# Pooling sums and most of the branch gating of a gated mixer on POOL instead of DVE

## The chip, the cores and the metric

One core of one Trainium2 chip (trn2) runs the whole program in a single launch. The metric is the time of an execution in device microseconds; of several runs the median is taken. The engines are named as in the profile: PE does the matrix products (its weight loads, PEld, run beside them), DVE and ACT are the two elementwise engines that can read PE's accumulators, POOL is the third elementwise engine, and SP issues most of the DMAs. Each engine takes its own instructions strictly in the order in which they stand in its queue, and waits for other engines by semaphores.

## The reference, cut to what matters

The model is two blocks on a sequence of 512 rows of 1024 numbers in fp32. The first (two layers of mixers, cross attention and a feed-forward net) isn't touched. The second has two layers; each is a mixer of three branches and a feed-forward net:

```
proj = h @ w_in[l]
q, k, v, f_logit, cx, cb, cc, px, gate_logit = split(proj)
y_attn = forgetting_attention(q, k, v, f_logit) @ w_attn_out[l]
y_conv = short_conv_mixer(cx, cb, cc, conv_w[l]) @ w_conv_out[l]
# pooling, for each of four groups of 64 features, window w = 2, 4, 8, 16:
#   d = (sum of the last w rows of px) / min(t + 1, w) - px
#   y_pool[group] = (d @ w_grp) * pool_scale
g = sigmoid(gate_logit)            # three gates of 1024 features
merged = g[0] * y_attn + g[1] * y_conv + g[2] * y_pool
x = x + merged @ w_o[l]
```

## The kernel before

Features lie on the 128 partitions and the 512 rows of the sequence along them, so a tile of 128 x 512 is 128 features of the whole sequence. Every product is done in three passes: both factors are split into a high part (rounded, by ACT, line 160) and a low part (the rest, by DVE, line 161), and PE adds high x high, high x low and low x high. So every block of weights that comes from memory costs ACT a cast and DVE a subtraction before PE can use it. The products with the large gate weights go by Strassen's scheme with seven products instead of eight (`seven`, `plan_seven`); that costs DVE four more additions of 128 x 1024 for each pair of blocks (line 469). A `Feed` keeps the splits of some four units of weights ahead of PE.

A layer's mixer (`mixer2`) runs attention heads first, with the short convolution's products between them, then:

- `pooling` (lines 1525 to 1559): the product for 256 features in two halves (`ft`). ACT copies a half out of the accumulator (`pu`, L1534). The window sums are built by doubling: `step` copies the first k columns and adds the tile to itself shifted by k (L1539, L1540). The first half (windows 2 and 4) needs two such steps, the second (8 and 16) four. Then follow a copy of 64 partitions (L1545, L1551), the division by the count (L1552 for the first 16 columns, L1553 for the rest) and the subtraction of the input (L1554). The result is split for the next product: the high part by ACT (L1558, two instructions of 64 partitions), the low part by DVE (L1559, two).
- `gates` (from line 1389): eight products of six matmuls each for the convolution's branch, whose accumulators ACT copies into `m` (L1440). Accumulators of this kind (tag `at`) have four buffers. Then `pool_conv` for each of four pairs of feature tiles: seven products for two gates, the sigmoids on ACT (L1456, L1444, L1445), the product of `m` with its gate (L1457), the pooled branch (two matmuls, L1454 and L1455, read by L1459) and its addition to `m` (L1461), the three of them on DVE. After the second and the fourth pair comes the attention branch (`attn`).

A scheduler orders the instructions of each engine by data dependences and by its own estimate of how long each takes; the program text alone does not set the order on ACT and DVE.

Of the kernel before, what the change touches and what calls it, by code (L numbers as in the profile page):

```python
# [15 lines left out]
ALU = mybir.AluOpType  # L16
# [5 lines left out]
S = 512  # L22
# [74 lines left out]
class Core:  # L97
# [1291 lines left out]
    def gates(self, mp, bt, l, w, aT, ds, ch, cl):  # L1389

        nc, a = self.nc, self.a
        v = nc.vector
        self.extra, self.turn = mp, 0

        self.T.append(mp.tile([P, 8, 256], F32R, name=self.nm("t4"), bufs=1))
        for i, (hi, lo) in enumerate(((self.Hh[:, 0:4, 256:], self.Hl[:, 0:4, 256:]),
                                      (self.T[2][:, 0:4, :], self.T[2][:, 4:8, :]))):
            b = self.block(mp, None, "rb").rearrange("p (k c) -> p k c", k=4)
            nc.sync.dma_start(out=b, in_=self.td[:, i])
            self.split(hi, lo, b)  # L1400

        ah = mp.tile([P, 4, S], F32R, name=self.nm("ah"), bufs=1)
        al = mp.tile([P, 4, S], F32R, name=self.nm("al"), bufs=1)
        mp.tile([P, 16], F32, name=self.nm("gap"), bufs=1)
        self.split(ah, al, aT)
        ms = [self.big(3), self.big(0)]
        m = [ms[f // 4][:, f % 4, :] for f in range(8)]
        feed = Feed()

        def src(g, fb, r):  # L1410
            c0 = 2568 + g * D + fb * 256
            return w[r * 512:r * 512 + 512, c0:c0 + 256]

        def pool_unit(fb):
            raw, hi, lo = [self.wp.tile([P, 1024], d, tag=t, name=self.nm("w"), bufs=n) for d, t, n in
                           ((F32, "raw", 3), (F32R, "whi", 5), (F32R, "wlo", 5))]
            for r in range(0, P, 64):
                nc.sync.dma_start(out=raw[r:r + 64, :256], in_=a["pool_w_2"][l, fb])
            self.split(hi[:, :256], lo[:, :256], raw[:, :256])
            return hi, lo  # L1420

        for fb in range(4):
            feed.put(lambda fb=fb: self.unit(a["w_conv_out_2"][l][:, fb * 256:fb * 256 + 256], 2, 256))
        for fb in range(4):
            feed.put(lambda fb=fb: pool_unit(fb))
            self.plan_seven(feed, mp, lambda i, r, fb=fb: src(1 + i, fb, r))
            if fb % 2:
                self.plan_seven(feed, mp, lambda i, r, fb=fb: src(0, fb - 1 + i, r))
                for i in range(2):
                    feed.put(lambda f=fb - 1 + i: self.unit(  # L1430
                        a["w_attn_out_2"][l][:, f * 256:f * 256 + 256], 4, 256))
        for i in range(4):
            feed.put(lambda i=i: self.unit(a["w_o_2"][l][i * 256:i * 256 + 256, 0:S], 2, S))

        for fb in range(4):
            u = feed.get()
            for c in range(2):
                p = self.at_tile()
                self.gemm_a(p, [u], c * P, ch, cl)
                nc.scalar.copy(out=m[fb * 2 + c], in_=p)  # L1440

        def second(a_, u):
            sg = bt.tile([P, S], F32, tag="sg", name=self.nm("sg"))
            nc.scalar.activation(out=sg[:, :256], in_=a_, func=AF.Sigmoid)  # L1444
            nc.scalar.activation(out=sg[:, 256:], in_=u, func=AF.Sigmoid)  # L1445
            return sg

        def pool_conv(fb):
            hi, lo = feed.get()

            def end(c, g, a_, u):
                f = fb * 2 + c
                p = self.at_tile()
                nc.tensor.matmul(p, lhsT=hi[:, c * P:(c + 1) * P], rhs=ds[:, fb, :], start=True, stop=False)  # L1454
                nc.tensor.matmul(p, lhsT=lo[:, c * P:(c + 1) * P], rhs=ds[:, fb, :], start=False, stop=True)  # L1455
                nc.scalar.activation(out=g, in_=g, func=AF.Sigmoid)  # L1456
                v.tensor_tensor(out=m[f], in0=m[f], in1=g, op=ALU.mult)  # L1457
                sg = second(a_, u)
                v.scalar_tensor_tensor(out=sg, in0=p, scalar=self.vec("psc", l * 8 + f), in1=sg,  # L1459
                                       op0=ALU.mult, op1=ALU.mult)  # L1460
                v.tensor_tensor(out=m[f], in0=m[f], in1=sg, op=ALU.add)  # L1461

            self.seven(feed, mp, end)

        def attn(fb, last):
            sgs = []

            def end(c, g, a_, u):
                nc.scalar.activation(out=g, in_=g, func=AF.Sigmoid)
                sgs.append((g, second(a_, u)))  # L1470

            self.seven(feed, mp, end)
            for i in range(2):
                un = feed.get()
                for c in range(2):
                    f = (fb + i) * 2 + c
                    p = self.at_tile()
                    self.gemm_a(p, [un], c * P, ah, al)
                    sg = sgs[c][i]
                    v.tensor_tensor(out=sg, in0=p, in1=sg, op=ALU.mult)  # L1480
                    v.tensor_tensor(out=m[f], in0=m[f], in1=sg, op=ALU.add)
                    if last:
                        self.split(self.Hh[:, f, :], self.Hl[:, f, :], m[f])

        for fb in range(4):
            pool_conv(fb)
            if fb % 2:
                attn(fb - 1, fb == 3)
        for f in range(4):
            self.split(self.Hh[:, f, :], self.Hl[:, f, :], m[f])  # L1490
        self.extra = None
        return [feed.get(5) for _ in range(4)]
# [32 lines left out]
    def pooling(self, bt, w, pool, ds):  # L1525

        nc = self.nc
        v = nc.vector
        us = self.units_a(w, 2312)
        for ft in range(2):  # L1530
            p = self.mm_tile()
            self.gemm_a(p, us, ft * P, self.Hh, self.Hl)
            u = bt.tile([P, S], F32, tag="cx", name=self.nm("pu"))
            nc.scalar.copy(out=u, in_=p)  # L1534
            s = bt.tile([P, S], F32, tag="sg", name=self.nm("psum"))
            s2 = bt.tile([P, S], F32, tag="sg", name=self.nm("cy"))

            def step(dst, src, k, lo):
                v.tensor_copy(out=dst[lo:, 0:k], in_=src[lo:, 0:k])  # L1539
                v.tensor_tensor(out=dst[lo:, k:], in0=src[lo:, k:], in1=src[lo:, :S - k], op=ALU.add)  # L1540

            if ft == 0:
                step(s, u, 1, 0)
                step(s2, s, 2, 64)
                v.tensor_copy(out=s[64:, :], in_=s2[64:, :])  # L1545
            else:
                step(s, u, 1, 0)
                step(s2, s, 2, 0)
                step(s, s2, 4, 0)
                step(s2, s, 8, 64)  # L1550
                v.tensor_copy(out=s[64:, :], in_=s2[64:, :])  # L1551
            v.tensor_tensor(out=s[:, :16], in0=s[:, :16], in1=pool[:, ft, :16], op=ALU.mult)  # L1552
            v.tensor_scalar(out=s[:, 16:], in0=s[:, 16:], scalar1=pool[:, ft, 16:17], scalar2=None, op0=ALU.mult)  # L1553
            v.tensor_tensor(out=s, in0=s, in1=u, op=ALU.subtract)  # L1554
            for e in range(2):
                r, o = slice(e * 64, e * 64 + 64), slice(64 - e * 64, 128 - e * 64)
                hi = ds[r, ft * 2 + e, :]
                nc.scalar.copy(out=hi, in_=s[r])  # L1558
                v.tensor_tensor(out=ds[o, ft * 2 + e, :], in0=s[r], in1=hi.bitcast(F32), op=ALU.subtract)  # L1559
# [162 lines left out]
```

## Time and profile before

| | us |
|---|---|
| median of three runs | 2978.25 (2976.13 to 2985.57) |
| the profiled execution's own time | 2976.68 |
| its span, first to last instruction | 2974.8 |
| PE busy | 2942.1 (99%) |
| DVE busy | 2259.5 (76%) |
| ACT busy | 1505.3 (51%) |
| POOL busy | 74.8 (3%) |

Times within the profile are counted from the first instruction. An engine's busy time is the time in which it had an instruction in work. Where a row ends in square brackets, these hold the idle time before it and what ended that. The second block's two mixers are alike: what stands at 1721 us in the first layer stands at 2425 us in the second.

### The profile page before, as it was taken

The page shows a single profiled execution, that of the slowest core. Times are in us where ns is not written, and L with a number is a line of the kernel's source. Part 1 is how long each engine was busy: PE and PEld are TensorE (multiplying, and loading weights), DVE is VectorE, ACT ScalarE, POOL GpSimd, SP SyncE. Part 2 cuts the span into 40 slices and gives each one's busy share as a digit, 9 for nine tenths or more (in the row PEclk, how much of TensorE's full clock was granted, in tenths as well). Part 3 has the DMA queues.
Part 4 walks back from the last instruction along what each step waited for, and adds up shares of the span by engine and source line. Part 5 has one row for each costly group of instructions (what it writes and reads, how often), then busy time and mean ns, then how long its engine had stood idle before and what let it go on. Part 6 is the DMA issues. An engine that isn't in the chain of part 4 may idle for free.

```text
span 2974.8 us, 46959 instructions
## 1 busy us (share of the span) xinstructions
PE 2942.1 (99%) x18312; PEld 2594.8 (87%) x18312; DVE 2259.5 (76%) x4266; ACT 1505.3 (51%) x2469; POOL 74.8 (3%) x113
## 2 busy tenths in 40 slices
PE   8999999999999999999999999999999999999999
PEld 6878889999988788999988789899998779999998
DVE  6855767988777576798879688697777778787775
ACT  6634545555444454555545465454444555454442
POOL 1300000000000000000001000000000000000000
PEclk9999999999999999999999999999999999999999
DMA  5122522343332353233335233423334324423332
GB/s 178 43 86 94 176 85 79 114 121 92 105 109 79 127 170 98 71 109 121 97 102 142 75 116 97 159 83 121 93 102 134 110 79 124 135 93 107 100 108 78
DMA packets 233955, 320.65 MB, mean 108 GB/s; under 512 B 11077, under 2 KB 166199, under 8 KB 232837
## 3 DMA queue, kind: packets, MB, share of 16 engines
q1 hardware_dynamic: 224933, 292.20, 31.5%
q0 software_dynamic: 8800, 25.45, 2.8%
q8 instruction: 144, 2.36, 0.3%
q14 instruction: 78, 0.64, 0.1%
HBM read 297.63 MB, written 15.78 MB: 105 GB/s over the span
## 4 chain that ended last, share of the span: by engine, by line
PE 88%; DVE 7%; ACT 2%; DMA 2%; issue 1%; SPq 0%; POOL 0%; DVEq 0%; ACTq 0%
PE mm L245 61%; PE at L245 19%; PE at L196 3%; DVE wl L161 2%; DVE wr L469 1%; PE at L1340 1%; DMA wr<-in_ffn_w_in 1%; DMA wr<-in_w_in 1%; PE at L1202 1%; ACT wh L160 1%; PE at L700 0%; PE at L857 0%; PE at L1624 0%; PE at L1626 0%; DVE x L548 0%
## 5 line engine op out<-in xcount | busy, mean ns | idle before, releaser
L161 DVE TENSOR_TENSOR wl<-wr,wh 128x1024 fp32r<-128x1024 f32 (+1 forms) x678 | 817.9, 1213 | 297.0 <-ACT wh L160 284.5
L160 ACT CAST wh<-wr 128x1024 fp32r<-128x1024 f32 (+1 forms) x678 | 702.4, 1044 | 581.5 <-PE mm L245 238.8
L245 PE MATMUL mm<-Hh,wh 128*128 128x256 f32 (+1 forms) x2256 | 678.1, 301 | 4.0 <-DVE g L518 3.7
L245 PE MATMUL mm<-Hh,wl 128*128 128x256 f32 (+1 forms) x2256 | 674.5, 299 | 0.0
L245 PE MATMUL mm<-Hl,wh 128*128 128x256 f32 (+1 forms) x2256 | 673.7, 299 | 0.0
L245 PEld LDWEIGHTS mm<-Hh,wh 128*128 128x128 f32 x2256 | 424.5, 188 | 24.1 <-DVE g L518 4.8
L245 PEld LDWEIGHTS mm<-Hl,wh 128*128 128x128 f32 x2256 | 425.4, 189 | 18.5
L245 PEld LDWEIGHTS mm<-Hh,wl 128*128 128x128 f32 x2256 | 424.9, 188 | 17.5 <-issue 0.3
L245 PE MATMUL mm<-wh,Hh 128*128 128x512 f32 x896 | 359.4, 401 | 0.8 <-ACT Hh L160 0.6
L245 PE MATMUL mm<-wl,Hh 128*128 128x512 f32 x896 | 354.1, 395 | 2.1 <-DVE ss L321 2.0
L245 PE MATMUL mm<-wh,Hl 128*128 128x512 f32 x896 | 353.8, 396 | 0.0
L245 PE MATMUL mm<-big,wh 128*128 128x256 f32 x1920 | 334.1, 277 | 1.7 <-DVE u L530 1.7
L245 PEld LDWEIGHTS mm<-big,wh 128*128 128x128 f32 x1920 | 289.6, 188 | 2.4 <-DVE u L530 2.3
L469 DVE TENSOR_TENSOR wr<-wr,wr 128x1024 f32<-128x1024 f32 x208 | 253.7, 1220 | 49.8 <-DMA wr<-in_w_ffn_in 25.2
L245 PE MATMUL at<-wh,al 128*128 128x512 f32 x704 | 277.4, 394 | 0.0
L245 PE MATMUL at<-wl,ah 128*128 128x512 f32 x704 | 276.1, 392 | 0.0
L245 PE MATMUL at<-wh,ah 128*128 128x512 f32 x704 | 273.8, 389 | 0.0
L245 PE MATMUL mm<-big,wl 128*128 128x256 f32 x960 | 265.6, 277 | 0.0
L245 PEld LDWEIGHTS mm<-wl,Hh 128*128 128x128 f32 x896 | 169.6, 189 | 38.0 <-DVE wl L161 3.3
L245 PEld LDWEIGHTS mm<-wh,Hl 128*128 128x128 f32 x896 | 169.3, 189 | 38.1 <-DVE Hl L161 1.3
L245 PEld LDWEIGHTS mm<-wh,Hh 128*128 128x128 f32 x896 | 169.4, 189 | 36.2 <-ACT Hh L160 1.2
L245 PEld LDWEIGHTS mm<-big,wl 128*128 128x128 f32 x960 | 180.2, 188 | 0.3 <-DVE wl L161 0.2
(403 smaller groups left out, 4268.2 us busy)
## 6 DMA issues: line engine op xcount, KB each, us to landing
wr<-in_ffn_w_in SPq DMA_DIRECT2D x88, 512.0 KB
wr<-in_w_ffn_in SPq DMA_DIRECT2D x88, 512.0 KB
wr<-in_w_in SPq DMA_DIRECT2D x84, 512.0 KB
wr<-in_ffn_w_out SPq DMA_DIRECT2D x44, 512.0 KB
wr<-in_w_ffn_out SPq DMA_DIRECT2D x44, 512.0 KB
wr<-in_ev_w_in SPq DMA_DIRECT2D x32, 512.0 KB
wr<-in_xa_w_kv SPq DMA_DIRECT2D x32, 512.0 KB
wr<-in_od_w_in SPq DMA_DIRECT2D x24, 512.0 KB
```

Source lines behind the costliest of these rows:

```text
L160: self.nc.scalar.copy(out=hi, in_=src)
L161: self.nc.vector.tensor_tensor(out=lo, in0=src, in1=hi.bitcast(F32), op=ALU.subtract)
L196: return self.nc.tensor.transpose(out=out, in_=in_, identity=self.ident)
L245: return self.nc.tensor.matmul(*args, **kw, skip_group_check=more)
L469: self.nc.vector.tensor_tensor(out=out, in0=a, in1=b, op=op)
L1202: nc.tensor.matmul(out[:, i * P:], lhsT=v[:, i, h * width:(h + 1) * width], rhs=pT[i], start=i == 0, stop=i == NT - 1)
L1340: last = self.chain(last, lambda: nc.tensor.matmul(po[e * 64:e * 64 + 64, i * P:], lhsT=vv[:, i, (h - 1 + e) * 64:(h + e) * 64], rhs=pair[ ...
```

## The change

Sixty-four instructions go from DVE to POOL, 32 in each layer: the 20 of `pooling` that build the sums, divide and subtract, and, for the first three of the four pairs, both gating instructions of each of the two feature tiles. The fourth pair's stay on DVE, and so do the splits and the instruction that reads the pooled branch's accumulator. In the changed file these lines stand one or two lines lower.

```
         def pool_conv(fb):
+            eng = nc.gpsimd if fb < 3 else v
...
                 nc.scalar.activation(out=g, in_=g, func=AF.Sigmoid)
-                v.tensor_tensor(out=m[f], in0=m[f], in1=g, op=ALU.mult)
+                eng.tensor_tensor(out=m[f], in0=m[f], in1=g, op=ALU.mult)
                 sg = second(a_, u)
                 v.scalar_tensor_tensor(out=sg, in0=p, scalar=self.vec("psc", l * 8 + f), in1=sg,
                                        op0=ALU.mult, op1=ALU.mult)
-                v.tensor_tensor(out=m[f], in0=m[f], in1=sg, op=ALU.add)
+                eng.tensor_tensor(out=m[f], in0=m[f], in1=sg, op=ALU.add)
...
+        g = nc.gpsimd
...
             def step(dst, src, k, lo):
-                v.tensor_copy(out=dst[lo:, 0:k], in_=src[lo:, 0:k])
-                v.tensor_tensor(out=dst[lo:, k:], in0=src[lo:, k:], in1=src[lo:, :S - k], op=ALU.add)
+                g.tensor_copy(out=dst[lo:, 0:k], in_=src[lo:, 0:k])
+                g.tensor_tensor(out=dst[lo:, k:], in0=src[lo:, k:], in1=src[lo:, :S - k], op=ALU.add)
...
-                v.tensor_copy(out=s[64:, :], in_=s2[64:, :])
+                g.tensor_copy(out=s[64:, :], in_=s2[64:, :])
...
-            v.tensor_tensor(out=s[:, :16], in0=s[:, :16], in1=pool[:, ft, :16], op=ALU.mult)
-            v.tensor_scalar(out=s[:, 16:], in0=s[:, 16:], scalar1=pool[:, ft, 16:17], scalar2=None, op0=ALU.mult)
-            v.tensor_tensor(out=s, in0=s, in1=u, op=ALU.subtract)
+            g.tensor_tensor(out=s[:, :16], in0=s[:, :16], in1=pool[:, ft, :16], op=ALU.mult)
+            g.tensor_scalar(out=s[:, 16:], in0=s[:, 16:], scalar1=pool[:, ft, 16:17], scalar2=None, op0=ALU.mult)
+            g.tensor_tensor(out=s, in0=s, in1=u, op=ALU.subtract)
```

The scheduler also sets ACT and DVE in another order. ACT before, in the first layer, from the last cast ahead of the pooling on (`psum_16843` and `psum_16884` are the two halves of the sums, `pu_16882` the second half's input, the `at` tiles the convolution's eight accumulators, `wh` the high parts of the next weights):

```order
L160 CAST Hh<-wr_16908 128x4x256
L160 CAST w_16964<-w_16963 128x256
L1534 COPY pu_16882<-mm_16857 128x512
L1440 COPY big_16921<-at_16947 128x512
L1558 CAST big_16799<-psum_16843 64x512 x2
L1440 COPY big_16921<-at_16955 128x512
L160 CAST wh_16994<-wr_16986 128x1024
L1440 COPY big_16921<-at_16970 128x512
L160 CAST wh_17014<-wr_16988 128x1024
L1440 COPY big_16921<-at_16978 128x512
L1440 COPY big_16922<-at_16998 128x512
L1440 COPY big_16922<-at_17006 128x512
```

ACT in the changed kernel, at the same place:

```order
L160 CAST Hh<-wr_16908 128x4x256
L1560 CAST big_16799<-psum_16843 64x512 x2
L160 CAST w_16964<-w_16963 128x256
L1536 COPY pu_16882<-mm_16857 128x512
L1440 COPY big_16921<-at_16947 128x512
L160 CAST wh_16994<-wr_16986 128x1024
L1440 COPY big_16921<-at_16955 128x512
L1440 COPY big_16921<-at_16970 128x512
L1560 CAST big_16799<-psum_16884 64x512 x2
L1440 COPY big_16921<-at_16978 128x512
L160 CAST wh_17014<-wr_16988 128x1024
L1440 COPY big_16922<-at_16998 128x512
```

The casts of the first half moved ahead of the copy of the second half's input; those of the second half, which stood behind all eight accumulator copies and two copies for the first gates, moved ahead of the fourth accumulator copy.

DVE before, in the first layer, from the last split ahead of the pooling's end on (`wl` are the low parts of the next weights):

```order
L161 TENSOR_TENSOR Hl<-wr_16908,Hh 128x4x256
L1554 TENSOR_TENSOR psum_16843<-psum_16843,pu_16841 128x512
L1539 COPY psum_16884<-pu_16882 128x1
L1540 TENSOR_TENSOR psum_16884<-pu_16882 128x511
L161 TENSOR_TENSOR w_16965<-w_16963,w_16964 128x256
L1559 TENSOR_TENSOR big_16799<-psum_16843,big_16799 64x512 x2
L469 TENSOR_TENSOR wr_17034<-wr_16990,wr_16992 128x1024
L1539 COPY cy_16885<-psum_16884 128x2
L1540 TENSOR_TENSOR cy_16885<-psum_16884 128x510
L161 TENSOR_TENSOR wl_16995<-wr_16986,wh_16994 128x1024
```

DVE in the changed kernel, at the same place:

```order
L161 TENSOR_TENSOR Hl<-wr_16908,Hh 128x4x256
L1561 TENSOR_TENSOR big_16799<-psum_16843,big_16799 64x512 x2
L161 TENSOR_TENSOR w_16965<-w_16963,w_16964 128x256
L469 TENSOR_TENSOR wr_17034<-wr_16990,wr_16992 128x1024
L469 TENSOR_TENSOR wr_16990<-wr_16986,wr_16990 128x1024
L161 TENSOR_TENSOR wl_16995<-wr_16986,wh_16994 128x1024
L1561 TENSOR_TENSOR big_16799<-psum_16884,big_16799 64x512 x2
L469 TENSOR_TENSOR wr_16986<-wr_17034,wr_16986 128x1024
L161 TENSOR_TENSOR wl_17015<-wr_16988,wh_17014 128x1024
```

The sums are gone from between the weights' work, and DVE's part of the second half's split (L1561, formerly L1559) moved up, ahead of the second unit of the next weights. PE's order is the same in both kernels.

## Rows read from the trace of the kernel before

**Rows 1.** Page, part 1: busy us (share of span) and instructions.

```profile
PE 2942.1 (99%) x18312; PEld 2594.8 (87%) x18312; DVE 2259.5 (76%) x4266; ACT 1505.3 (51%) x2469; POOL 74.8 (3%) x113
```

**Rows 2.** Timeline of PE, first layer: start, us, engine, line, what, [idle before].

```profile
1747.28 0.39 PE L245 MATMUL mm<-Hh,wh 128*128 128x256 f32 x1 [1.31 <-DVE g L518]
...
1766.46 0.39 PE L245 MATMUL mm<-x,wl 128*128 128x256 f32 x1 [1.28 <-DVE wl L161]
```

**Rows 3.** Waits of PE, second layer, 2400 to 2590: total us, times, longest.

```profile
PE mm L245 <- DVE wl L161: 1.5, 2, 1.0
PE mm L245 <- DVE g L518: 1.4, 1, 1.4
PE mm L245 <- ACT u L526: 0.3, 1, 0.3
PE mm L245 <- DVE u L530: 0.3, 1, 0.3
```

**Rows 4.** Instructions by line, DVE, whole span: ns min/median/max, first and last start.

```profile
L1457 DVE TENSOR_TENSOR big<-big,g x16: 679/684/687, 1759.1 to 2558.2; 128x512 f32<-128x512 f32 x16
...
L1540 DVE TENSOR_TENSOR cy<-psum x6: 677/682/684, 1722.2 to 2440.0; 64x510 f32<-64x510 f32 x2, 128x510 f32<-128x510 f32 x2, 64x504 f32<-64x504 f32 x2
```

**Rows 5.** POOL: two lines by duration, then its timeline.

```profile
L868 POOL TENSOR_TENSOR z<-lf x16: 610/728/1593, 58.8 to 135.7; 128x256 f32<-128x256 f32 x16
L872 POOL TENSOR_TENSOR z<-z,key x16: 731/942/3168, 68.0 to 137.5; 128x256 f32<-128x256 f32 x16
...
0.75 0.10 POOL L119 MEMSET ones<- 128x2 f32 x1 [0.29 <-POOLq L1710]
...
24.54 0.72 POOL L712 CAST mask<-mf 128x640 uint8<-128x640 f32 x1 [22.42 <-DMA mf<-in_c_hgmask]
...
79.26 0.69 POOL L868 TENSOR_TENSOR z<-lf 128x256 f32<-128x256 f32 x1 [0.34 <-POOL z L868]
```

**Rows 6.** Timeline of POOL and DVE, first block, 77 to 108.

```profile
77.76 0.69 DVE L881 TENSOR_TENSOR qd<-qd,big 128x512 f32<-128x512 f32 x1
...
78.16 0.77 POOL L868 TENSOR_TENSOR z<-lf 128x256 f32<-128x256 f32 x1 [0.67 <-ACT kd L880]
78.36 1.11 DVE L882 TENSOR_TENSOR kd<-kd,key 128x512 f32<-128x512 f32 x1
...
104.55 3.87 POOL L872 TENSOR_TENSOR z<-z,key 128x256 f32<-128x256 f32 x2 [3.16 <-ACT z L869]
104.77 2.35 DVE L161 TENSOR_TENSOR wl<-wr,wh 128x1024 fp32r<-128x1024 f32 x2
```

**Rows 7.** Timeline of ACT, first layer, 1724 to 1738.

```profile
1725.84 0.41 ACT L160 CAST w<-w 128x256 fp32r<-128x256 f32 x1 [0.36 <-PE mm L245]
1726.15 0.58 ACT L1534 COPY pu<-mm 128x512 f32<-128x512 f32 x1
1727.47 0.59 ACT L1440 COPY big<-at 128x512 f32<-128x512 f32 x1 [0.74 <-PE at L245]
1728.69 1.26 ACT L1558 CAST big<-psum 64x512 fp32r<-64x512 f32 x2 [0.63 <-DVE psum L1554]
```

**Rows 8.** Timeline of DVE, first layer, 1719 to 1733.

```profile
1719.14 2.29 DVE L161 TENSOR_TENSOR al<-big,ah 128x2048 fp32r<-128x2048 f32 x1 [4.24 <-ACT ah L160]
...
1724.04 1.22 DVE L161 TENSOR_TENSOR t<-wr,t 128x1024 fp32r<-128x1024 f32 x1 [1.15 <-ACT t L160]
...
1725.75 0.69 DVE L161 TENSOR_TENSOR wl<-wr,wh 128x512 fp32r<-128x512 f32 x1
...
1726.84 1.22 DVE L161 TENSOR_TENSOR Hl<-wr,Hh 128x1024 fp32r<-128x1024 f32 x1
...
1729.23 0.42 DVE L161 TENSOR_TENSOR w<-w,w 128x256 fp32r<-128x256 f32 x1
...
1731.12 1.23 DVE L469 TENSOR_TENSOR wr<-wr,wr 128x1024 f32<-128x1024 f32 x1
```

**Rows 9.** Timeline of PE, first layer: the eighth product, then the first gate's.

```profile
1735.67 0.63 PE L245 MATMUL at<-big,wh 128*128 128x512 f32 x2
...
1737.07 0.28 PE L245 MATMUL mm<-Hh,wh 128*128 128x256 f32 x1
1737.19 0.28 PE L245 MATMUL mm<-Hl,wh 128*128 128x256 f32 x1
```

**Rows 10.** Waits of PE, whole span, the attention stages': total us, times, longest.

```profile
PE at L1624 <- ACT pT L1218: 1.7, 2, 0.8
```

**Rows 11.** Windows: us, busy by engine (instructions), PEclk, DMA share, GB/s.

```profile
1665.20:1672.00 6.80, 6.80 (x21) 5.83 (x22) 5.38 (x18) 2.14 (x8) 0.54 (x1) 0.50 0.10 30
```

More of the change, by code (lines that the diff above doesn't have):

```diff
@@ L1550, in pooling @@
                 step(s2, s, 8, 64)
-                v.tensor_copy(out=s[64:, :], in_=s2[64:, :])
-            v.tensor_tensor(out=s[:, :16], in0=s[:, :16], in1=pool[:, ft, :16], op=ALU.mult)
-            v.tensor_scalar(out=s[:, 16:], in0=s[:, 16:], scalar1=pool[:, ft, 16:17], scalar2=None, op0=ALU.mult)
-            v.tensor_tensor(out=s, in0=s, in1=u, op=ALU.subtract)
+                g.tensor_copy(out=s[64:, :], in_=s2[64:, :])
+            g.tensor_tensor(out=s[:, :16], in0=s[:, :16], in1=pool[:, ft, :16], op=ALU.mult)
+            g.tensor_scalar(out=s[:, 16:], in0=s[:, 16:], scalar1=pool[:, ft, 16:17], scalar2=None, op0=ALU.mult)
+            g.tensor_tensor(out=s, in0=s, in1=u, op=ALU.subtract)
             for e in range(2):
```

## Prediction

> **What bounds the kernel now.** Read the busy times first: TensorE is busy for 2942.1 of 2974.8 us [rows 1], so an edit pays only where PE stands still, and costs whatever it adds to that. DVE's 76% says nothing by itself. The change touches two stretches, one in each layer of the second block: the pooling sums (from 1721 and 2425 us) and the gating that follows (to some 1860 and 2560 us). So the second view is who PE waited for there. In the first layer there are two waits of 1.3 us, before 1747.28 and 1766.46, both for DVE [rows 2]; in the second 3.5 us in all, for DVE but for 0.3 [rows 3]. **All that can be won is 2.6 + 3.5 = 6.1 us, 0.2% of the time.** A measurement of this kernel tells some 0.3% (9 us) from no change, so a measurable gain is out of reach, and the question is what the change costs. For that the third view is needed, the timelines of ACT, DVE and PE around the pooling, because ACT and DVE are handed POOL's result in the middle of their queues.
>
> **What leaves DVE.** 24 gating instructions of 0.684 us, 12 shifted additions of 0.68 [rows 4], and the four subtractions and the copies and scalings between them: over 27 us in all. Since PE waited for DVE only in the 6.1 us above, the rest was hidden, and frees nothing.
>
> **What POOL takes for them.** Nothing of 512 columns with two inputs runs on POOL before. The nearest rows are its 128x256 instructions: 0.61 for a subtraction and 0.73 for a product at the least [rows 5]. Twice that is 1.22 to 1.46 us; I take 1.3, nearer the subtraction, as all eight of this width in a layer's sums add or subtract. (By the Trainium skill, GPSIMD Engine Reference, section 3.1, an addition of 2048 columns takes 4497 ns; a quarter, 1.12 us, would be an estimate somewhat under my lower end, and would take some 3 us off the whole forecast.) A copy or a scaling of 512 columns: 0.72 x 512/640 = 0.57, from the CAST. A tiny copy: 0.15, the smallest MEMSET being 0.10. Most steps read what the step before wrote and wait for POOL's own signal: between 0 and the 0.34 that stands before one of its instructions [rows 5]; I take 0.1, since that is a single row.
> - First half (two shifted additions, one subtraction; one copy and one scaling of some 500 columns; two tiny copies and a scaling of 16 columns): 3 x 1.3 + 2 x 0.57 + 3 x 0.15 + 4 x 0.1 = 5.9 us. Ends: 5.1 and 7.3.
> - Second half (two more additions, each with its tiny copy): 5 x 1.3 + 2 x 0.57 + 5 x 0.15 + 6 x 0.1 = 9.0 us. Ends: 7.7 and 11.2.
>
> **Contention.** Where both engines read two tiles, the records stretch: POOL's 0.61 became 0.77 and the DVE instruction behind it 1.11, where its twin just before took 0.69; and two POOL products beside two splits on DVE took 3.87 [rows 6]. So POOL's sums also wait for the DVE work that is ready at the time, or the reverse. (The Trainium skill, SBUF — State Buffer, section "Who interferes with whom", has it as an exclusive lock: a DVE instruction with two SBUF inputs and a POOL instruction that reads SBUF block one another, the later one wholly. The rows agree: 1.11 is 0.69 and two thirds of POOL's 0.61. Without such a lock the two terms 2.8 and 3.9 below would be 0, and the forecast 13 us less.)
>
> **Where it lands on the path.** All times are of the first layer. The order shows two things: on ACT the two casts of the first half stand ahead of the copy of the second half's input, and the casts of the second half ahead of the fourth of eight copies that empty the convolution's accumulators (L1440). PE's order is unchanged, and these accumulators have four buffers (line 105), so the eighth product cannot start until the fourth copy is done.
> - POOL can start when DVE's 128x2048 split ends, at 1721.4 [rows 8]. It needs 5.9 us, and during its later half DVE has three splits ready (1.22, 0.69, 1.22 from 1724.04 on). As every step of the sum waits for the last, DVE's waiting instruction gets in between; I add 2.8 of the 3.1 (ends 0 and 3.1). First half done: 1721.4 + 5.9 + 2.8 = **1730.1** (1726.5 to 1731.8).
> - ACT then does its two casts (1.26) and the cast and copy that took from 1725.84 to 1726.73 before [rows 7]: 2.2 us. The second half's input, there at 1726.73 before, is there at 1732.3.
> - POOL's second half: 9.0 us, beside DVE's 0.42 + two 1.23 + one 1.22 = 4.1 us of ready work [rows 8], of which I add 3.9 (ends 0 and 4.1): done at **1745.2** (1736.4 to 1749.3).
> - Until then ACT stands at the casts and DVE at its own part of the split. Behind ACT's wait are the copy of the fourth accumulator, four more such copies and every cast of the next weights; behind DVE's, the sums and splits of those weights. When POOL is done: two casts (1.26) and the copy (0.59), so the eighth product starts 1.9 later, at **1747.1**. Before, the first of its six matmuls started at 1735.67 [rows 9]. PE is 11.4 us late (2.6 to 15.5).
> - The next weights cost nothing more: their cast ends 1 us after the fourth copy, and their split 2.7 us after it, while PE still has the eighth product (1.4 us) and one ready unit (24 matmuls at 0.118 from one start to the next, 2.8 us [rows 9]) before it needs them.
>
> **What comes back.** After that stall PE is the late one, so the wait for L518 at 1746 (1.3 us) should be gone: -1.3. The second wait, at 1765, lies behind gating instructions on DVE; four of them (2.7 us) leave, and PE comes later, so I count it as gone: -1.3. The gating on POOL itself I count as hidden: its products are read again only in the attention part, POOL's queue holds nothing else until the next layer's loads, and only the buffer g is wanted earlier, by ACT's first copy for the next pair (L513); if that cover fails, it is the second rival.
>
> **The clock.** In the attention stage, after matmuls of 128 columns and waits of up to 0.8 us [rows 10], the granted clock was 0.50 for 6.8 us [rows 11], that is 1.2 instead of 2.4 GHz, which costs 3.4 us of progress. A stall of 11 us will hardly leave the clock up; part of the slow time falls into the stall. I take +2.5 (0 to 3.4).
>
> **Sum.** A layer: 11.4 - 1.3 - 1.3 + 2.5 = +11.3 us; the second layer has the same order, so +22.4 for both with its somewhat larger waits. The profiled execution took 2976.68 (span 2974.8 and 1.9 around it): 2999.1. The median of the three runs lies 1.6 higher, hence **3001**. The lower ends give 2.6 - 2.6 = 0 a layer, the upper ones 15.5 - 1.3 + 3.4 = 17.6, 35 in all.
>
> **Rivals.**
> - *The sums are quick, and nothing waits* (the other side). If POOL ran these steps at DVE's speed and DVE's work stayed out of their way, the second half would end before 1733.8 (1735.67 less 1.9), and that is the point from which it decides. Then PE stalls nowhere and the 6.1 us come back: 2972. With POOL at my lower ends and without contention PE is late by 2.6 and wins it back: 2978 to 2982. For it: POOL is idle there, and ACT's and DVE's waits empty the field for it. Against it: the two halves at their lowest, with ACT's 2.2 between, take 15.0 us from 1721.4, which is 1736.4, too late already. Chance 0.15, nearly all of it within 0.3%.
> - *The gating costs too.* Four POOL instructions for each pair of features take 4.9 to 5.8 us; if they hold DVE back for all of it, DVE has 2.2 to 3.1 us more to do there than before, not 2.7 less. At 1765 PE already waits for DVE, so there it shows at once: six such places at 2.2 to 3.1, 3001 + 13 to 18 = 3014 to 3019. (By the SBUF page of the Trainium skill this is what two saturated engines should do to one another.) Against it: a waiting POOL instruction can use DVE's idle time, nobody needs its result soon, and PE is late by then. Chance 0.08.
> - *Forecast:* ACT's queue stalls PE at the eighth product, 2988 to 3014. Chance 0.75. The 0.02 left is a gain that I don't see.
>
> **How the numbers follow.** Faster by over 0.3% 0.02; within 0.3% 0.14, the first rival; slower 0.84. The range takes the forecast with both ends but for the last corner of the low one, half of the second rival, and the upper part of the first: 2983 to 3016.
>
> **What would show it.** After: a PE wait of about 10 us in each layer before the eighth accumulator (for ACT's L1440 copy), near 1736 and 2439; ACT idle 9 to 12 us before the second pair of casts, released by POOL's subtraction; POOL's shifted additions at 1.2 to 1.5 us when alone and longer beside DVE; the clock at 0.50 behind the stall; the waits for L518 gone. I am wrong if POOL's second half takes under 8 us including its waits, or if PE's wait there is under 3 us.

## The result, and the profile after

The changed kernel takes 3007.5 us (median of 4, 3002.3 to 3014.1) against 2978.3 for the kernel before beside it: a ratio of 1.0104 (95% interval 1.0086 to 1.0122), so slower by some 1%, and 6.5 us above the forecast of 3001. The profiled execution took 3011.71 (span 3009.9). Of the lines named below, L1440 is the same in the changed file, L1457 is L1458 there and L1558 is L1560.

PE's waits, engine and line waited for, us in total, times, longest us, first in the first layer, then in the second; they answer to [rows 2, 3]:

```profile
PE at L245 <- ACT big L1440: 10.0, 2, 8.9
PE mm L245 <- DVE g L518: 4.7, 4, 1.4
...
PE at L245 <- ACT big L1440: 10.0, 2, 8.9
PE mm L245 <- DVE g L518: 3.2, 4, 1.3
PE mm L245 <- DVE u L530: 1.2, 1, 1.2
```

Before, these stretches held 2.6 and 3.5 us of waits. Now PE waits 8.9 us once in each layer for a copy on ACT and 1.0 once. It also waits at four L518 additions a layer where the kernel before had no wait (the one of before, at 1747.28 in the first layer, is gone): some 1.2 us each in the first layer, 0.8 in the second, which has one of 1.2 for L530 besides. ACT in the first layer around the long wait (start us, us, instruction, idle before and what ended it):

```profile
1732.67 1.26 ACT L1560 CAST big<-psum 64x512 fp32r<-64x512 f32 x2 [4.62 <-POOL psum L1556]
1733.96 0.41 ACT L160 CAST w<-w 128x256 fp32r<-128x256 f32 x1
1734.27 0.58 ACT L1536 COPY pu<-mm 128x512 f32<-128x512 f32 x1
...
1746.88 1.26 ACT L1560 CAST big<-psum 64x512 fp32r<-64x512 f32 x2 [9.62 <-POOL psum L1556]
1748.16 0.58 ACT L1440 COPY big<-at 128x512 f32<-128x512 f32 x1
```

ACT stands at its casts for 9.62 us, until POOL's last subtraction; right behind them is the copy that frees the accumulator. PE at the eighth product, in the same view:

```profile
1739.48 0.39 PE L245 MATMUL at<-big,wl 128*128 128x512 f32 x1
1748.80 0.80 PE L245 MATMUL at<-big,wh 128*128 128x512 f32 x1 [8.92 <-ACT big L1440]
```

Whole program, before [rows 1] against after: DVE lost 64 instructions, which took 33.5 us in the trace of before (16.4 the gating's 24, 17.1 the 40 of the sums; the prediction's "over 27" was low), yet its busy time fell by only 8.0.

```profile
PE 2953.8 (98%) x18312; PEld 2604.9 (87%) x18312; DVE 2251.5 (75%) x4202; ACT 1504.8 (50%) x2469; POOL 162.4 (5%) x177
```

**Layer by layer.** PE runs the same 18312 matmuls in the same order in every kernel here, so the start of the same matmul can be compared. From the first product of the convolution's branch to the last of the gating, the first layer's stretch grew by 15.8 us and the second's by 13.6, 29.4 together; the medians differ by 29.2. In code that didn't change the profiled execution drifted by +2.7 us ahead of the first stretch, -2.7 between the two and +5.8 behind the second; single executions differ so. This measure is called "stretch" below.

A stretch also takes in something that is no wait. At a granted clock of 1.00, matmuls of 256 columns follow each other at 0.113 us in some places and at 0.118 in others, in every kernel here. In the first layer of the run with the sums alone it is 0.118 throughout, which costs 2.8 us against before from 1775 us on, where PE waits in neither kernel. The cause is open, so differences of up to 3 us between stretches are compared with the waits below.

### The profile page after: what moved, and what is told of

Its sections match the earlier page's. It is cut to its first block, busy times and chain, and to the rows that moved or that the text cites. A ratio compares the mean times of both kernels' runs of the same rounds, so it can differ in the third digit from the quotient of the medians.

```text
span 3009.9 us, 47041 instructions
## 1 busy us (share of the span) xinstructions
PE 2953.8 (98%) x18312; PEld 2604.9 (87%) x18312; DVE 2251.5 (75%) x4202; ACT 1504.8 (50%) x2469; POOL 162.4 (5%) x177
## 5 line engine op out<-in xcount | busy, mean ns | idle before, releaser
L161 DVE TENSOR_TENSOR wl<-wr,wh 128x1024 fp32r<-128x1024 f32 (+1 forms) x678 | 833.2, 1235 | 297.8 <-ACT wh L160 288.6
```

What stands on the lines that cost most here:

```text
L161: self.nc.vector.tensor_tensor(out=lo, in0=src, in1=hi.bitcast(F32), op=ALU.subtract)
```

## The experiments

"Sums" are the 20 POOL instructions of `pooling` in a layer, "gating" the 12 of `pool_conv`. The stretches, in us against before, and the ratio of times to before with its 95% interval:

| kernel | stretch, layer 1 | layer 2 | both | ratio (interval) |
|---|---|---|---|---|
| after (sums and gating on POOL) | 15.8 | 13.6 | 29.4 | 1.0104 (1.0086, 1.0122) |
| sums only | 12.5 | 8.2 | 20.7 | 1.0060 (1.0036, 1.0083) |
| gating only | 8.8 | 8.7 | 17.5 | 1.0061 (1.0045, 1.0077) |
| idle work on POOL, two inputs | 8.9 | 9.1 | 18.0 | 1.0061 (1.0037, 1.0085) |
| idle work on POOL, one input | 4.3 | 2.4 | 6.7 | 1.0021 (1.0010, 1.0032) |
| sums only, scaling on DVE | 5.6 | 8.2 | 13.7 | 1.0046 (1.0025, 1.0066) |
| sums, second cut behind the copies | 8.5 | 5.3 | 13.8 | 1.0039 (1.0024, 1.0054) |
| sums, second cut late | 2.0 | 2.2 | 4.2 | 1.0010 (0.9998, 1.0023) |
| sums, both cuts late | 3.3 | 1.8 | 5.1 | 1.0016 (0.9999, 1.0034) |
| sums, cuts at two places | 1.9 | 0.0 | 1.9 | 1.0008 (0.9995, 1.0021) |
| sums and their split on POOL | 3.1 | 3.7 | 6.9 | 1.0016 (0.9997, 1.0036) |
| sums and gating, second cut late | 6.8 | 6.6 | 13.4 | 1.0045 (1.0031, 1.0060) |

"Cut" means the casts and subtractions that split POOL's result (L1560, L1561).

**Sums only, gating only.** The change taken apart.

```diff
-            eng = nc.gpsimd if fb < 3 else v
+            eng = v                      # sums only
```

For gating only, `eng` stays as changed and `pooling` is the one of before.

> Only the pooling sums go to POOL; the gating stays on DVE. Theory (ACT's queue stalls PE): the sums alone make the stall at the eighth product, so PE's waits for ACT L1440 stay as in the changed kernel (10.0 us a layer, longest 8.9), with 3.1 us of low clock behind them, and the four L518 waits of the gating (4.7 and 3.2 us a layer) go. By the decomposition of the changed kernel that is 10.0 + 3.1 - 2.6 = +10.5 us in the first layer and +9.6 in the second, so 2998. Rival (the gating's waits only follow from the stall, or DVE's extra 2.7 us a pair keep them): L518 waits of 3 us and more a layer stay, and the time is that of the changed kernel, 3007. Rival (the sums cost nothing once DVE is not disturbed by the gating): 2978.

> Only the gating of three of four pairs goes to POOL; the sums stay on DVE. Theory (two engines on one memory port): DVE's 128x1024 instructions beside POOL's take 1.7 to 2.0 us instead of 1.22, and PE waits for L518 behind them though no stall came before: four new waits of about 1.2 us a layer, of which one takes the place of the old wait at 1765 (1.3), so +3.4 a layer and 2985; more, up to 2990, if the stall of the changed kernel had given DVE time. ACT's L1440 waits are 0. Rival (gating on POOL is hidden, as the prediction counted it): no L518 wait behind POOL's gating, one wait fewer than before, 2976.

PE's waits in the first layer, sums only and then gating only:

```profile
PE at L245 <- ACT big L1440: 10.0, 2, 8.9
```

```profile
PE mm L245 <- DVE g L518: 7.3, 5, 3.0
PE mm L245 <- ACT sg L1444: 1.5, 1, 1.5
PE mm L245 <- DVE wl L161: 0.7, 1, 0.7
PE mm L245 <- DVE u L530: 0.3, 1, 0.3
```

The sums alone make the whole L1440 stall and next to nothing else: 2997.4 us, as expected (2998); the stretches, 12.5 and 8.2, lie on either side of the 10.5 and 9.6 worked out for it, the first with the 2.8 us of slower matmuls in it. The gating alone makes no L1440 wait but costs about as much, 2997.4, where 2985 to 2990 were expected: 9.8 us of waits in the first layer, the longest 3.0, while of the old ones of 2.6 [rows 2] 2.1 stayed. So the gating was not hidden at all. The two parts add to 38.2 us of stretch, more than the change's 29.4.

**Idle work on POOL.** Everything stays on DVE as before; POOL only does work that nobody reads.

```diff
                 v.tensor_tensor(out=m[f], in0=m[f], in1=g, op=ALU.mult)
+                if fb < 3:
+                    nc.gpsimd.tensor_tensor(out=idle, in0=g, in1=g, op=ALU.mult)
...
                 v.tensor_tensor(out=m[f], in0=m[f], in1=sg, op=ALU.add)
+                if fb < 3:
+                    nc.gpsimd.tensor_tensor(out=idle, in0=sg, in1=sg, op=ALU.add)
```

> The kernel before, with all its work on DVE, and beside each gating instruction of the first three pairs one more of the same shape on POOL, started by the same sigmoid or by the pooled branch's product, whose result nothing reads. Theory (memory port): POOL's instructions stretch DVE's 128x1024 ones to 1.7 to 2.0 us, and as DVE also keeps its twelve gating instructions a layer (8.2 us in all), the L518 waits are at least those of the gating-only kernel: 5 to 8 us a layer more than before, 2988 to 2994. Rival (the waits come from handing data from ACT and DVE to POOL and back, not from the port): nobody waits for these results, so the time stays at 2978 and DVE's 128x1024 instructions at 1.22 us.

> As the run with idle instructions on POOL beside the gating on DVE, but POOL only copies g and sg (one input of 128x512) instead of combining two inputs. Theory (POOL's reads and DVE's two-input instructions exclude one another, for as long as POOL's instruction lasts): a copy of 64x512 took 0.61 us alone where an addition of 512 columns took 1.03, so DVE's 128x1024 splits beside them take 1.22 + 0.6 = 1.8 us, and the cost is some 60% of the 9 us a layer of the two-input run: 2986 to 2989. Rival (it takes two inputs on either side): the splits stay at 1.22 and the time at 2976. Rival (any POOL instruction started there costs the same): 2995.

In the second run `tensor_copy(out=idle, in_=g)` and `in_=sg` stand in their place. DVE in the first layer beside POOL's two-input idle work, and beside its copies (L1459 and L1465 are the two gating instructions, both still on DVE):

```profile
1762.96 0.68 DVE L1459 TENSOR_TENSOR big<-big,g 128x512 f32<-128x512 f32 x1
1763.56 1.53 DVE L1465 TENSOR_TENSOR big<-big,sg 128x512 f32<-128x512 f32 x1
1765.01 0.74 DVE L1463 SCALAR_TENSOR_TENSOR sg<-at,pv,sg 128x512 f32<-128x512 f32 x1
```

```profile
1762.19 1.21 DVE L469 TENSOR_TENSOR wr<-wr,wr 128x1024 f32<-128x1024 f32 x1
1763.32 1.09 DVE L1465 TENSOR_TENSOR big<-big,sg 128x512 f32<-128x512 f32 x1
```

An instruction of 0.68 us takes 1.53 beside POOL's two-input work and 1.09 beside a POOL copy. DVE's busy time grew by 16.5 us over before with the 24 two-input instructions, 5.3 with the 24 copies: 0.69 and 0.22 each. Nobody needs POOL's results here, and still the stretches grew by 18.0 and 6.7 us. With the two-input work ACT waited once a layer, for 0.6 us, until POOL had read a `g` buffer; with the copies nobody waited for POOL. That shows contention as a cause by itself; handing data over isn't needed for it. Not all of the 18.0 is waiting: the clock was low for 3.4 and 6.8 us in these stretches. The places differ from what was expected: in the first layer 3.4 us of waits for L518, 2.4 for wl and 1.1 for a cast, not all at L518, and DVE's 128x1024 instructions were stretched less than 1.7 to 2.0 (1.22 and 1.24 in the mean from 1765 to 1800), since much of the contention fell on its own gating (1.53 in the mean there). The two-input run took 2995.7 us, above the 2988 to 2994 expected. The copies' price was expected at 60% of that of the two-input work and came to 37% (6.7 of 18.0): 2984.8 us, under the 2986 to 2989 expected and clear of 2976, the rival in which copies cost nothing.

**The place of the casts in ACT's queue.** Four kernels with the sums on POOL and the gating on DVE. In each of them the cut is a function that `gates` calls at a later place, with its casts queued behind a named ACT instruction:

```diff
+            def cut(s=s, ft=ft):
+                for e in range(2): ...        # the casts and subtractions, unchanged
...
+        with self.tc.issue_after(last.ins):   # last: the ACT copy that it is queued behind
+            cut()
```

> The sums on POOL and the gating on DVE, as in the run with the sums alone, but the casts and subtractions that take POOL's results (L1560, L1561 of the changed kernel) are queued on ACT behind the third product of the first gating pair, at about 1748 us of the first layer, when POOL is long done. Theory (it is the place in ACT's queue, not POOL's speed): the L1440 waits fall from 10.0 us a layer to under 0.5, the low clock behind them goes, and the old waits for L518 and wl (2.6 and 3.5 us) shrink, since DVE has lost the sums: 2972 to 2979. Rival (POOL's time itself is on the path, or its use of the port slows DVE's splits): a wait of 3 us or more stays between 1725 and 1750 and the time is over 2986.

> Sums on POOL, gating on DVE; only the second half's casts and subtractions are queued late (behind the third product of the first gating pair), the first half's stay where the changed kernel has them, so that POOL's second half isn't held up by a buffer, as it was for 17.3 us in the run with both late. Theory (place in the queue): of the L1440 waits only the 1.0 us before the fifth product is left, the waits of before for L518 and wl go, the 4.5 us wait for the run with both late (DVE standing at the late subtraction) goes too, since POOL is done at about 1744: 1.0 - 2.6 and 1.0 - 3.5 a layer, so 2972 to 2976, against 2997 with the same work in the other order. Rival (POOL's second half is late wherever its result is wanted): a wait of 3 us or more for DVE or ACT between 1740 and 1760, 2982 or more.

> Sums on POOL, gating on DVE; the first half's casts and subtractions behind the fourth copy of the convolution's accumulators (L1440), the second half's behind the third product of the first gating pair. Theory (place in the queue): no L1440 wait at all, and the old waits of 2.6 and 3.5 us gone, as DVE has lost the sums: 2970 to 2974, at most 0.2% faster than before. Rival (the late first half holds up POOL's second half by its buffer, as in the run with both late): a wait for L535 or L1440 of some 2 to 4 us, 2978 to 2984.

> Sums on POOL, gating on DVE; the second half's casts and subtractions are queued right behind the eighth L1440 copy, between the place of the changed kernel (stall 8.9 us) and that of the run with the second cut late (none). Theory (ACT's place in the queue sets the stall): ACT reaches the casts at about 1737, waits until POOL is done at about 1744 and is free at 1745.3; behind it stand a weights cast and the first L513 copies, which PE needs for the third gate product, 5.6 us after 1737.1: a wait of 2.5 to 4 us for ACT L513 (or a weights cast) instead of L1440, no low clock of 10 us, 2980 to 2985. Rival (POOL's speed sets it, wherever the casts stand): 8 us or more, 2994 or more.

In all four L1440's 8.9 us wait is gone, with POOL doing the same work; but all four took longer than their theories said (2982.4 us with both cuts late, 2983.5 with the second late, 2981.9 with the cuts at two places, 2992.9 with the second behind the copies). First layer, second cut late:

```profile
PE at L245 <- ACT big L1443: 1.0, 1, 1.0
PE mm L245 <- ACT g L513: 0.9, 1, 0.9
PE mm L245 <- DVE u L533: 0.8, 1, 0.8
PE mm L245 <- ACT g L522: 0.3, 1, 0.3
```

Only the 1.0 us from the first half's cut is left of the stall (L1443 is L1440 there). But the old waits were replaced by others, not removed: 3.0 us against 2.6, 4.5 against 3.5 in the second layer, and no gain: the interval of the ratio takes in 1, as it does with both cuts late and at two places. With *both* cuts late a wait of 4.5 us for L535 (L538 there) came, where DVE stood at the second half's late subtraction; POOL's own queue shows why that half was late:

```profile
1728.80 1.03 POOL L1546 TENSOR_TENSOR psum<-pu 128x511 f32<-128x511 f32 x1
1747.16 0.19 POOL L1545 COPY cy<-psum 128x2 f32<-128x2 f32 x1 [17.33 <-DVE big L1567]
```

The second half's `cy` needs a buffer that the first half's sums hold until they are split, so the late first cut held POOL's second half for 17.3 us (7.4 with the cuts at two places, the rival there; PE's longest wait in that kernel is 1.7 us, which the profile puts down to no engine).

The run with the second cut right behind the copies missed: PE waited 7.2 us for L513 instead of 2.5 to 4. POOL in its second half, the shifted additions only:

```profile
1738.91 2.03 POOL L1544 TENSOR_TENSOR psum<-pu 128x511 f32<-128x511 f32 x1
...
1742.03 2.02 POOL L1544 TENSOR_TENSOR cy<-psum 128x510 f32<-128x510 f32 x1
...
1745.14 2.02 POOL L1544 TENSOR_TENSOR psum<-cy 128x508 f32<-128x508 f32 x1
...
1748.26 2.25 POOL L1544 TENSOR_TENSOR cy<-psum 64x504 f32<-64x504 f32 x1
```

The expectation took POOL's end from the changed kernel, 1744. There DVE stood still too and left POOL alone: its third addition took 1.03. Here DVE went on with its splits, each of POOL's four took 2.0 or more, and the half took 16.6 us (1738.63 to 1755.2) instead of 11.9. So the stall shortened itself: with DVE standing still POOL was faster, and taking the waiting instructions out of the way makes POOL slower.

**The split on POOL too.** The program's order is untouched; ACT and DVE have nothing that waits for POOL.

```diff
-                nc.scalar.copy(out=hi, in_=s[r])
-                v.tensor_tensor(out=ds[o, ft * 2 + e, :], in0=s[r], in1=hi.bitcast(F32), op=ALU.subtract)
+                g.tensor_copy(out=hi, in_=s[r])
+                g.tensor_tensor(out=ds[o, ft * 2 + e, :], in0=s[r], in1=hi.bitcast(F32), op=ALU.subtract)
```

> As the run with the sums alone, with the program's order untouched, but the casts and subtractions of POOL's results (L1560, L1561) are POOL instructions too, so that nothing in ACT's or DVE's queue waits for POOL. POOL does some 3 us more work in each half. Theory (ACT's head of queue makes the stall): no L1440 wait and no low clock of 10 us; POOL is done at about 1748 to 1751, before the pooled branch's first matmul at 1754: 2974 to 2982, like the two runs with late cuts. Rival (POOL's work, of which there is now more, sets the stall): a wait over 9 us, 2998 or more. Rival (port): DVE's splits are stretched by the added instructions, 3 us of L518 or wl waits a layer, 2984.

No L1440 wait is left, though POOL's work grew and its second half came 9 us later than in the changed kernel (its scaling starts at 1755.2 against 1744.0, with the first product 2.3 us later): 2982.4 us, at the upper edge of what was expected, with 4.3 us of shorter waits in the first layer, these and two of 0.3:

```profile
PE mm L245 <- ACT g L513: 1.5, 1, 1.5
PE mm L245 <- DVE u L530: 1.4, 2, 0.8
PE mm L245 <- DVE wl L161: 0.8, 1, 0.8
```

With the late cuts this settles that the stall is one of queue order: ACT waiting at its casts with an accumulator's copy behind them. (DVE's part of the cut moved along each time; that ACT's part makes the stall is read from the trace, where PE's wait ends with L1440.) POOL was done much later than the 1748 to 1751 expected, with its split at 1764.8, behind the pooled branch's first matmul at 1763.3. No matmul needed it by then: the second half's split is read from the third pair on (`ds[:, fb, :]`; L1454 at 1829 in the kernel before). What is wanted sooner is the buffer of its sums, whose tag `sg` the gating's tiles share.

**The scaling on DVE.**

```diff
-            g.tensor_scalar(out=s[:, 16:], in0=s[:, 16:], scalar1=pool[:, ft, 16:17], scalar2=None, op0=ALU.mult)
+            v.tensor_scalar(out=s[:, 16:], in0=s[:, 16:], scalar1=pool[:, ft, 16:17], scalar2=None, op0=ALU.mult)
```

> As the run with the sums alone, but the scaling by the count (L1555, 128x496) stays on DVE. It prices the one POOL step that the prediction had far too low (0.57; measured 3.0 us in the first half, 1.5 in the second). Theory (POOL's chain is the path to the stall, step by step): the first half is some 2.2 us shorter, with a DVE instruction and two handings-over in place of 3.0, the second 1.0, and PE's longest L1440 wait falls from 8.9 to 5.5 to 6 us: 2997 less 6 to 8, 2989 to 2991. Rival (the scaling only fills time that contention takes anyway, and DVE's queue holds it up): the wait stays at 8.5 us or more, 2996 or more.

First layer:

```profile
PE at L245 <- ACT big L1440: 6.0, 1, 6.0
```

PE's longest wait for L1440 fell from 8.9 to 6.0 us, as expected, and the one of 1.0 went too: so the queue's order makes the stall, and the length of POOL's chain sets its size. The time was 2991.7 us, just above what was expected. The stretches do not show it so plainly: the first fell by 6.9 us, 2.8 of them the slower matmuls of the run it is compared with, and the second not at all, since a wait of 2.0 for L530 and a low clock of 3.4 us came at its end.

**Sums and gating, second cut late.** Does the stall hide part of the gating's cost?

> The changed kernel, sums and gating on POOL, with only the second half's casts and subtractions queued late. It asks why the gating cost 8.8 us a layer alone but the whole change 15.8 and 13.6 rather than 12.5 + 8.8 and 8.2 + 8.7. Theory (the stall gave DVE time to get ahead, which hid part of the gating's cost): with the stall gone the waits of the gating come back to those of the gating-only run, 7 us and more of L518 waits a layer, against 4.7 and 3.2 in the changed kernel: 2976 + 2 x 8.8 less up to 4 = 2990 to 2995. Rival (the gating costs 4.5 us a layer whenever the sums are on POOL, because DVE has lost the sums too): L518 waits of 3 to 5 us a layer, 2980 to 2985.

First layer:

```profile
PE mm L245 <- DVE g L518: 5.0, 4, 1.6
PE mm L245 <- DVE wl L161: 1.1, 1, 1.1
PE at L245 <- ACT big L1443: 1.0, 1, 1.0
PE mm L245 <- ACT g L513: 0.9, 1, 0.9
```

The time, 2992.8, lies where the theory put it, but the waits are the rival's: 5.0 and 4.4 us for L518, not 7 and more. Against the same kernel with the gating on DVE the stretches grew by 13.4 - 4.2 = 9.2; in the changed kernel the gating added 29.4 - 20.7 = 8.7. All of PE's waits together grew by 5.2 and 4.1 us in the two layers here (8.2 against 3.0, 8.6 against 4.5), and by 4.7 and 4.0 in the changed kernel (14.7 against 10.0, 14.4 against 10.4). So the gating costs about the same with and without the stall, and the theory is wrong. Alone it added 7.2 us of waits in the first layer, but 4.7 in the second, whose stretch of 8.7 also holds 6.8 us at the low clock. So it is dearer alone in part only, and that DVE then has the sums to do as well is one possible reason, which no run separates. Why one wait at the end of the second pair is 3.0 us long there and 1.3 here is open.

## Why the prediction was right, and where it wasn't

**The mechanism of the forecast** was the one that happened, at the place it named: ACT idle 9.6 us at the second pair of casts (9 to 12 forecast), PE waiting for L1440 before the eighth product, in both layers, and the low clock behind it. The runs with the casts elsewhere or on POOL show that ACT's queue is the cause.

**The terms for the first layer**, forecast and measured. In the changed kernel the first product starts 2.7 us later than before, so absolute times are less 2.7:

| step | forecast | measured |
|---|---|---|
| POOL's first half done | 1730.1 | 1729.9 |
| from there to the second half's input | 2.2 | 2.3 |
| second half, with contention | 12.9 | 11.9 |
| eighth product late | 11.4 | 10.4 |
| low clock | 2.5 | 3.1 |
| old waits that go | -2.6 | -2.6 |
| gating on POOL | 0 | 4.7 |
| layer | 11.3 | 15.6 of 15.8 |

The low clock is counted as half of the low stretch behind the wait's end, 6.2 us here; the gating by PE's waits. The second layer: of its low stretch only 3.4 us lay behind the wait's end, so 10.4 + 1.7 - 3.5 + 4.4 = 13.0, measured 13.6.

**POOL's steps** came out at the right sum from wrong parts. First layer, two steps of the first half, then the second half:

```profile
1727.19 1.08 POOL L1554 TENSOR_TENSOR psum<-psum,poolc 128x16 f32<-128x16 f32 x1
1728.25 3.01 POOL L1555 TENSOR_SCALAR psum<-psum,poolc 128x496 f32<-128x496 f32 x1
...
1735.19 2.03 POOL L1542 TENSOR_TENSOR psum<-pu 128x511 f32<-128x511 f32 x1
1737.28 1.07 POOL L1541 COPY cy<-psum 128x2 f32<-128x2 f32 x1
...
1740.39 0.19 POOL L1541 COPY psum<-cy 128x4 f32<-128x4 f32 x1
1740.54 1.03 POOL L1542 TENSOR_TENSOR psum<-cy 128x508 f32<-128x508 f32 x1
...
1743.97 1.52 POOL L1555 TENSOR_SCALAR psum<-psum,poolc 128x496 f32<-128x496 f32 x1
1745.58 1.26 POOL L1556 TENSOR_TENSOR psum<-psum,pu 128x512 f32<-128x512 f32 x1
```

A shifted addition takes 1.03 to 1.05 alone (the last, 64x504, 1.25), under the lower end of 1.22 taken from [rows 5]; the subtraction 1.26 to 1.29, within it. (The estimate from the Trainium skill, GPSIMD Engine Reference, section 3.1, was 1.12, nearer for the additions than the rows.) The scaling takes 1.52 alone and 3.0 in the first half beside two splits, where 0.57 was taken from a CAST: a scaling by a value per partition is not a copy on POOL. The run with the scaling on DVE took 2.9 us off PE's longest wait. Additions too dear by 0.2 to 0.3 and a scaling too cheap by 1.0 nearly cancel in the sum. That the first half came out to 0.2 us is in part luck.

**Contention** was taken for POOL's sums as 2.8 and 3.9 us. It measured some 2.4 (0.9 at the 16 columns, 1.5 at the scaling) and 2.9. In the second half a tiny copy and the additions beside DVE's 1.22 us instructions grew from 0.19 to 1.07 and from 1.03 to 2.03, by nearly a DVE instruction each. But DVE was soon at its own part of the cut and out of the way, so the second half ran alone after 1740.

**The step that failed** is that the gating on POOL is hidden. The forecast put it at 0: it priced only POOL's side and the buffers, though it used the contention of [rows 6] for the sums a few lines above, and left contention in the gating to a rival with a chance of 0.08. Its sign "the waits for L518 gone" did not come: the old one went and four others came. DVE and POOL in the first layer behind the first pair:

```profile
1771.74 2.00 DVE L469 TENSOR_TENSOR wr<-wr,wr 128x1024 f32<-128x1024 f32 x1
1773.66 0.73 DVE L1460 SCALAR_TENSOR_TENSOR sg<-at,pv,sg 128x512 f32<-128x512 f32 x1
1774.33 3.91 DVE L161 TENSOR_TENSOR wl<-wr,wh 128x1024 fp32r<-128x1024 f32 x2
1778.16 0.74 DVE L1460 SCALAR_TENSOR_TENSOR sg<-at,pv,sg 128x512 f32<-128x512 f32 x1
1778.82 3.45 DVE L161 TENSOR_TENSOR wl<-wr,wh 128x1024 fp32r<-128x1024 f32 x2
1782.19 0.74 DVE L518 TENSOR_TENSOR g<-mm,g 128x256 f32<-128x256 f32 x2
```

```profile
1771.09 3.82 POOL L1458 TENSOR_TENSOR big<-big,g 128x512 f32<-128x512 f32 x2 [24.25 <-ACT g L1457]
1774.86 2.29 POOL L1462 TENSOR_TENSOR big<-big,sg 128x512 f32<-128x512 f32 x1
1779.04 2.14 POOL L1462 TENSOR_TENSOR big<-big,sg 128x512 f32<-128x512 f32 x1 [1.90 <-DVE sg L1460]
```

DVE's five 128x1024 instructions take 9.4 us there instead of 6.1: 3.3 more, against four gating instructions of 0.68, 2.7, that left. So DVE reaches L518 later than if it had kept them, and PE waits 1.18 us. In the gating-only run DVE lost 24 instructions (16.4 us) and its busy time grew by 7.3: 23.7 us of stretching, 1.0 for each POOL instruction. That is the mechanism of the second rival, as it was put. It gave 2.2 to 3.1 at six places (three a layer), and what came was some 1.2 at four places in the first layer and 0.9 at five in the second: 4.7 and 4.4 us for its 6.6 to 9.3.

DVE's L1460, which reads an accumulator and one tile, stayed at 0.73 beside POOL's L1458, while instructions that read two tiles were stretched. (The Trainium skill, SBUF — State Buffer, section "Who interferes with whom", has it so: outside its two-port modes, a DVE instruction with at most one SBUF input doesn't contend with POOL, and one with two contends with a POOL instruction that reads SBUF. The rows agree, and for one input on POOL's side too: DVE's 0.68 became 1.09 beside a POOL copy.)

**The sum.** Forecast 22.4 for both layers, measured 29.4; the difference of 7.0 is the gating (9.1 by its waits) less the smaller terms. (By the prediction's own waits, 3.5 in the second layer, its sum would be 21.7.) The measured 3007.5 also lies within the forecast's own ends, 2988 to 3014. They were that wide for POOL's steps and its contention in the sums, and the stall came out near the middle; that there was room left for the gating, which the forecast had at nothing, was luck.

**The first rival**, that nothing waits, needs POOL done by 1733.8; it was done at 1744.1. The 6.1 us that could be won were not won by any version either: the four with the sums on POOL, the gating on DVE and no wait of over 5 us ran at 1.0008 to 1.0016 times before, with 1 inside each interval.

## What to carry to other kernels

Before an instruction goes to a slower engine, look at which in-order queues are handed its result in their middle, and what stands behind the waiting instruction: here one accumulator copy behind two casts made 8.9 us of PE's wait, and moving the casts and subtractions to a later place, or onto POOL, removed it. DVE work given to POOL while DVE is busy can come back on DVE when both read SBUF tiles: price it by what it adds to DVE's neighbours, here 1.0 us for each gating instruction of 0.68 that left. With the sums most of it did leave: in the run with the sums alone DVE's busy time fell by 12.2 of 17.1 us, in part because DVE stood waiting beside them. And with the bound engine at 99%, add up its waits first: 6 us was the most that this change could win.

## What the runs showed of the hardware that wasn't expected

- Contention goes both ways and feeds back: POOL's second half took 11.9 us where DVE stood waiting for it, and 16.6 where DVE went on.
- TensorE's granted clock was 0.50, the 1.2 GHz level, from within each wait of 6 us and more on, and from 0.6 us behind the end of the two of 4.5. The stretch that answers to [rows 11]:

```profile
1744.80:1755.00 10.20, 6.20 (x23) 5.63 (x24) 7.29 (x7) 7.65 (x12) 1.96 (x2) 0.50 0.03 3
```

  With waits of 8.9 us it was low for 10.2 us in both layers of two kernels; with 6.0 (scaling on DVE) for 6.8; with 4.5 (both cuts late) for 3.4; with 7.2 and 7.3 for 10.2 in one layer and 6.8 in the other. Stretches with several waits of 1 to 3 us had between none and 6.8 of it. Of the 10.2 us 6.2 lay behind the wait's end in the stretch shown, 3.4 in the second layer of the same kernel. The low stretch of [rows 11], at the same code in the kernel before, is missing in the changed kernel and came in some executions of the others only, so that one seems to belong to the execution and not to the change.
- On POOL a scaling by a value per partition (128x496) takes 1.52 us, more than a shifted addition or a subtraction of that width (1.03 to 1.29).
